# Latent heads inside a decoder trunk: the value slice moves from ScalarE to VectorE, the squares are formed from the copy, and the copy gets a third buffer

## The chip, the cores and the metric

One core of a Trainium2 chip runs the whole program. A core has a matrix engine (TensorE, PE in the profile), a vector engine (VectorE, DVE), an activation engine (ScalarE, ACT) and a general one (GpSimd, POOL). Each works through its own list of instructions in order. They share an SBUF memory; matrix products land in PSUM, in banks of 128 partitions x 512 float32. DMA transfers are issued by SyncE (SP) and by ACT, each from its own queue, and run on 16 shared DMA engines. The metric is the device time of one execution in microseconds (us); lower is better.

## The reference

The reference is a trunk of four layers over 1024 tokens of width 1024 plus 16 meta tokens. The even layers hold two groups of eight attention heads side by side: latent heads, whose queries and keys come out of a low-rank compression, and forgetting heads. What the change touches is the head of the latent group, cut here:

```
q  = (rms_norm(c_q,  g_cq)  @ w_uq ).reshape(b, l, 8, 96)          # c_q  384 wide
kv = (rms_norm(c_kv, g_ckv) @ w_ukv).reshape(b, l, 8, 64 + 64)     # c_kv 256 wide
k_nope, v_mla = kv[..., :64], kv[..., 64:]
k  = concatenate([k_nope, broadcast(k_pe, 8 heads)], axis=-1)      # 96 wide
q  = rope_tail(rms_norm(q, g_q_mla), cos, sin)
k  = rope_tail(rms_norm(k, g_k_mla), cos, sin)
```

So for each token and head there is a product, a sum of squares over the head's columns, a scaling by its inverse root, and a rotation of the last 32 columns. The values are scaled by the latent norm alone. After the attention comes one output projection, then the MLP or convolution layers, which fill the rest of the time.

## The kernel before

The attention of the even layer runs head by head. `prep(h)` loads a head's operands: for a forgetting head `fox_prep` (L406) issues on SP a query tile, a key tile, two halves of a second key tile (all from `fop_d`, L410 to L413) and a row of decay terms copied to all partitions (from `frow_d`, L414), all into tiles named `op`. `softmax` (L451) lets PE write scores into a bank named `sc` (L72 is the helper that records every matmul), DVE take them out with the running minimum (L474), ACT form exponentials with their sum (L484), DVE the reciprocal of the sum (L485) and GpSimd the scaling (L486). `transposes` (L491) turns blocks of 128 x 128 on PE into bank `tr` (L505), which DVE (L509) or ACT (L511) copies out into `pt`; `values` (L515) multiplies by the values into bank `av`, and ACT copies that out and stores it in two DMAs (L527 to L532). There are three `sc` banks, three `tr` banks, one `av` bank and one bank named `pq`.

`latent_heads` (L569) is a generator. While the first seven forgetting heads are worked on (270 to 480 us), it is resumed between their pieces, at a rate set by a constant, so that its matmuls stand between theirs on PE. It goes twice over nine token tiles (eight of 128 tokens, one of 16): pass 0 makes the queries (3 blocks of the latent, 4 heads x 96 = 384 columns a group), pass 1 keys and values (2 blocks, 512 columns). For each token tile `turn` loads a piece of the latent on SP (L588, `cn`), transposes it on PE (L591) and splits it into a high part on ACT (L595, `cH`) and a remainder on DVE (L596, `cL`). Then come two groups per tile ("quads"). A group is 9 or 6 matmuls into the one `pq` bank, out of weights `mwH` and `mwL`. ACT then squares the bank into `mjk` (L619), copies it into `qk` (L620) and in pass 1 scales the value half into `vv` (L622); DVE sums the squares (L624). After both groups a short chain on DVE and ACT (L627 to L638; L630 and L631 on ACT) forms the inverse roots, GpSimd scales and rotates `qk` in place (L636 to L653), and ACT's DMA queue stores `qk` (L654) and `vv` (L641). The `qk` and `vv` tiles have two buffers: a tile can be written again when the store of two tiles back has landed.

The latent heads then load what was stored: `tokens` (L388 to L391) reads `qk_d` into tiles `tm` and `v_d` into `v` on SP. After them the output projection begins: `w_out` (L673) loads a block of weights (`woraw`), DVE casts it (L678, `woH`), and PE multiplies in `pq` banks.

The order on every engine is not the order of the code. A scheduler places all instructions by its own simulated timeline, so an edit in one generator moves instructions of other functions too. Each DMA is also given one of eight completion lanes in turn, over both queues, and waits until the lane's last transfer has landed; in the listings these are the waits named DMAHW.

Of the kernel before, what the change touches and what calls it, by code (L numbers as in the profile page):

```python
# [18 lines left out]
F32 = mybir.dt.float32  # L19
BF16 = mybir.dt.bfloat16  # L20
F32R = mybir.dt.float32r
AF = mybir.ActivationFunctionType
ALU = mybir.AluOpType
# [4 lines left out]
P = 128  # L28
# [38 lines left out]
def trunk(ctx: ExitStack, tc: tile.TileContext, a: dict, out: bass.AP):  # L67
    nc = tc.nc
    V, S, G, T = nc.vector, nc.scalar, nc.gpsimd, nc.tensor
# [39 lines left out]
    with ExitStack() as att:  # L109
# [5 lines left out]
        lat = ac.tile([P, 2, NTT], F32, name="lat")  # L115
# [23 lines left out]
        with ExitStack() as s1:  # L139
# [90 lines left out]
            def project(i, WH, WL, N):  # L230
                t0, m = TT[i]
                ps = bank("sc")[:m, :N]
                n = 0
                for k in range(KD):
                    for x, w in ((H, WH), (H, WL), (L, WH)):
                        mm(ps, x[k][:, t0:t0 + m], w[k], n == 0, n == 23)
                        n += 1
                return ps
# [11 lines left out]
            for i, (t0, m) in enumerate(TT):  # L250
                ps = part[i] if i < 7 else project(i, *W, 296)
# [28 lines left out]
            j = fp.tile([P, NTT, 32], F32, name="pesq", bufs=1)  # L280
# [11 lines left out]
            for i, (t0, m) in enumerate(TT):  # L292
                ps = project(i, *W, NQL)
# [13 lines left out]
            for i0, i1 in ((0, 4), (4, 8), (8, 9)):  # L307
                ps = bank("tr")
                n = 0
                for i in range(i0, i1):  # L310
                    m = TT[i][1]
# [31 lines left out]
            for w in range(2):  # L343
                W = weights(f"w_g{2 + w}", 512)
                for i, (t0, m) in enumerate(TT):
                    ps = project(i, *W, 512)
                    j = jk.tile([P, 512], F32, name="jk")[:m]
# [7 lines left out]
                    x = jk.tile([P, 512], F32, name="cr")[:m].rearrange("p (h d) -> p h d", d=64)  # L355
# [10 lines left out]
            for i, (t0, m) in enumerate(TT):  # L366
                ps = project(i, *W, 512)
                if late:
                    turn(*late.pop(0))
                x = jk.tile([P, 512], F32, name="cr")[:m]  # L370
# [198 lines left out]
        def latent_heads():  # L569
            with ExitStack() as st:  # L570
                mw = st.enter_context(tc.tile_pool(name="mw", bufs=2, reuse_waits="tile"))
                for which, (k0, K, d) in enumerate(((0, 3, 96), (3, 2, 64))):
# [27 lines left out]
                    for i, (t0, m) in enumerate(TT):  # L600
                        if i + 1 < NTT:
                            turn(i + 1)
                            yield
                        cH, cL = cs_[i]
                        qk = mw.tile([P, 8, 96], F32, name="qk")[:m]
                        ss = small.tile([P, 8], F32, name="mss")[:m]
                        if which:
                            vv = mw.tile([P, 512], F32, name="vv")[:m]
                        for quad in range(2):
                            ps = bank("pq")[:m, :n4]  # L610
                            n = 0
                            for k in range(K):
                                for x, w in ((cH, WH), (cH, WL), (cL, WH)):
                                    mm(ps, x[:, k], w[:, k, quad * n4:quad * n4 + n4], n == 0, n == 3 * K - 1)
                                    n += 1
                            hs = slice(4 * quad, 4 * quad + 4)
                            x = ps[:, :4 * d].rearrange("p (h d) -> p h d", d=d)
                            j = mw.tile([P, NQL], F32, name="mjk")[:m, :4 * d].rearrange("p (h d) -> p h d", d=d)
                            S.activation(out=j, in_=x, func=AF.Square)  # L619
                            S.copy(out=qk[:, hs, :d], in_=x)  # L620
                            if which:
                                S.activation(out=vv[:, 256 * quad:256 * quad + 256], in_=ps[:, 256:512], func=AF.Copy,  # L622
                                             scale=lat[:m, 1, i:i + 1])
                            V.tensor_reduce(out=ss[:, hs], in_=j, axis=AX.X, op=ALU.add)  # L624
                            yield

                        V.tensor_scalar(out=ss, in0=ss, scalar1=lat2[:m, which, i:i + 1], scalar2=spe[:m, which, i:i + 1],  # L627
                                        op0=ALU.mult, op1=ALU.add)
                        y, t, rr = [small.tile([P, 8], F32, name="m" + n)[:m] for n in "ytr"]
                        S.activation(out=y, in_=ss, func=AF.Ln)  # L630
                        S.activation(out=y, in_=y, func=AF.Exp, scale=-0.5)  # L631
                        V.tensor_tensor(out=t, in0=y, in1=y, op=ALU.mult)
                        V.tensor_tensor(out=t, in0=t, in1=ss, op=ALU.mult)
                        V.tensor_scalar(out=t, in0=t, scalar1=-0.5, scalar2=1.5, op0=ALU.mult, op1=ALU.add)
                        V.scalar_tensor_tensor(out=rr, in0=y, scalar=lat[:m, which, i:i + 1], in1=t, op0=ALU.mult, op1=ALU.mult)
                        G.tensor_tensor(out=qk[:, :, :d], in0=qk[:, :, :d], in1=rr.unsqueeze(2).broadcast_to([m, 8, d]), op=ALU.mult)  # L636
                        if which:
                            V.tensor_tensor(out=rr, in0=y, in1=t, op=ALU.mult)  # L638
                            G.tensor_tensor(out=qk[:, :, 64:96], in0=kpe[:m, i, :].unsqueeze(1).broadcast_to([m, 8, 32]),
                                            in1=rr.unsqueeze(2).broadcast_to([m, 8, 32]), op=ALU.mult)  # L640
                            nc.scalar.dma_start(out=v_d[1].rearrange("r p i d -> p r i d")[:m, :, i],  # L641
                                                in_=vv.rearrange("p (r d) -> p r d", d=P))
                        else:
                            x1, x2 = qk[:, :, 64:80], qk[:, :, 80:96]
                            tb = [tab[0][:m, i, n, :].unsqueeze(1).broadcast_to([m, 8, 16]) for n in range(4)]
                            t1 = mw.tile([P, 8, 16], F32, name="t1")[:m]
                            t2 = mw.tile([P, 8, 16], F32, name="t2")[:m]
                            G.tensor_tensor(out=t1, in0=x2, in1=tb[2], op=ALU.mult)
                            G.tensor_tensor(out=t2, in0=x1, in1=tb[3], op=ALU.mult)
                            G.tensor_tensor(out=x1, in0=x1, in1=tb[0], op=ALU.mult)  # L650
                            G.tensor_tensor(out=x2, in0=x2, in1=tb[1], op=ALU.mult)
                            G.tensor_tensor(out=x1, in0=x1, in1=t1, op=ALU.subtract)
                            G.tensor_tensor(out=x2, in0=x2, in1=t2, op=ALU.add)  # L653
                        nc.scalar.dma_start(out=qk_d[which].rearrange("h p i d -> p h i d")[:m, :, i], in_=qk)  # L654
                        yield
# [96 lines left out]
        for m in PAIRS[:4]:  # L752
            x = op_.tile([P, 342], F32, name="hf", bufs=6)
            nc.scalar.dma_start(out=x, in_=h_d[m][:, 0:342])
            first[m] = x
        for n, m in enumerate(first):
            w = w_out(m, 0)
            ps = bank(("sc", "pq", "sc", "sc")[n])[:, :342]
# [28 lines left out]
    def bank_(w):  # L787
        return mp.tile([P, 512], F32, name="mp")[:, :w]
# [194 lines left out]
    for m in PAIRS:  # L983
        w = w_out(m, 0)
        for c0, c1 in ALL[m in first:]:
            ps = bank_(342)
# [232 lines left out]
```

## Time and profile before

| | |
|---|---|
| median of 3 runs | 2543.8 us (2543.32 to 2549.25) |
| the profiled execution | 2543.92 us, span 2542.2 us |
| mean granted TensorE clock | 0.982 |
| PE busy | 2428.5 us, 96% of the span |
| DVE, ACT, POOL busy | 1571.7, 807.8, 920.0 us |
| the latent stage, 270 to 480 us | PE busy 190.1 of 210, DVE 146.3, ACT 122.5, POOL 97.6 |

A row of the timeline gives the start, the duration, engine, line, operation, what is written and read, and in brackets the idle time of the engine just before and what ended it. "ACTq" and "SPq" rows are DMA issues on those queues. The duration of a matmul includes its latency, so matmuls that follow each other are read by the distance of their starts. A row of one line or tile gives the count and the least, median and greatest duration in nanoseconds. Rows of the DMA view give the number of transfers, the size of each and the time from issue to landing.

### The profile page before, as it was taken

How to read it: one execution, taken by the hardware profiler on the slowest of the kernel's cores; microseconds unless marked ns; L12 is line 12 of the kernel's file. 1: busy time of each engine (PE TensorE's matmuls, PEld its weight loads, DVE VectorE, ACT ScalarE, POOL GpSimd, SP SyncE). 2: the span in 40 equal slices, each digit the busy share in tenths (PEclk: the TensorE clock that was granted, in tenths of full speed). 3: DMA queues.
4: the chain of work that ended last, by engine and by line, in shares of the span. 5: the costliest groups of instructions: out<-in, count | busy, mean ns of one | idle time of the engine just before them, and what ended most of it. 6: DMA issues, size and time to landing. Idle time of an engine off the chain costs nothing.

```text
span 2542.2 us, 39452 instructions
## 1 busy us (share of the span) xinstructions
PE 2428.5 (96%) x15182; PEld 2162.6 (85%) x15182; DVE 1571.7 (62%) x3049; ACT 807.8 (32%) x1651; POOL 920.0 (36%) x694
## 2 busy tenths in 40 slices
PE   7999889999986999999999979999989999999999
PEld 7877676789886999999999969998868888888889
DVE  8573667665769666654544588778696556553432
ACT  3222456554635333320100252221353333210100
POOL 6353344532313333342423214445333334342420
PEclk9999999999998999999999989999999999999999
DMA  5234545444142333372312212225314334531311
GB/s 158 80 114 134 164 133 158 140 136 126 57 172 76 110 106 105 106 242 75 133 67 100 67 59 67 67 67 177 114 67 133 108 109 127 211 126 67 117 57 67
DMA packets 165645, 285.95 MB, mean 112 GB/s; under 512 B 35720, under 2 KB 104776, under 8 KB 165456
## 3 DMA queue, kind: packets, MB, share of 16 engines
q1 hardware_dynamic: 88608, 217.86, 26.8%
q10 hardware_dynamic: 76848, 65.56, 7.9%
q8 instruction: 120, 1.97, 0.3%
q14 instruction: 69, 0.57, 0.1%
HBM read 198.45 MB, written 84.91 MB: 111 GB/s over the span
## 4 chain that ended last, share of the span: by engine, by line
PE 79%; DVE 9%; DMA 6%; issue 4%; ACT 1%; POOL 1%; SPq 0%; ACTq 0%; DVEq 0%; POOLq 0%
PE mp L72 32%; PE mp L918 29%; PE sc L72 8%; PE pq L72 3%; PE av L72 3%; PE tr L505 3%; DVE lp L1143 1%; DMA qk_d<-qk 1%; DMA lp<-w_in_conv 1%; PE tr L439 1%; DMA lp<-w_up 1%; DVE hgL L178 1%; DVE pg L812 0%; DVE pg L809 0%; PE tr L333 0%
## 5 line engine op out<-in xcount | busy, mean ns | idle before, releaser
L918 PE MATMUL mp<-pg,lp 128*128 128x256 f32 (+2 forms) x5976 | 882.6, 310 | 39.9 <-ACT wk L941 10.7
L918 PEld LDWEIGHTS mp<-pg,lp 128*128 128x128 f32 x5976 | 818.1, 191 | 104.6 <-ACT wk L941 10.9
L72 PE MATMUL mp<-pg,lp 128*128 128x342 f32 (+2 forms) x4416 | 812.8, 346 | 0.7 <-DVE pg L1035 0.7
L72 PEld LDWEIGHTS mp<-pg,lp 128*128 128x128 f32 x4416 | 734.8, 189 | 77.8 <-DVE pg L1035 1.0
L910 POOL TENSOR_TENSOR lp<-lp 128x512 fp32r<-128x512 f32 x216 | 309.8, 1443 | 603.1 <-ACT lp L909 602.2
L1057 DVE TENSOR_TENSOR pg<-pg,mp 128x342 f32<-128x342 f32 (+2 forms) x368 | 206.8, 570 | 366.4 <-PE mp L72 366.2
L1046 POOL TENSOR_TENSOR lp<-lp 128x1024 fp32r<-128x1024 f32 x72 | 185.1, 2571 | 444.9 <-PE mp L72 382.4
L909 ACT CAST lp<-lp 128x512 fp32r<-128x512 f32 x303 | 179.3, 617 | 412.9 <-DVE lp L895 262.2
L1034 ACT CAST pg<-pg 128x1024 fp32r<-128x1024 f32 (+1 forms) x72 | 75.8, 1053 | 531.9 <-DMA pg<-hid 488.9
L486 POOL TENSOR_SCALAR Sb<-Sb,ls 128x144 f32<-128x144 f32 (+7 forms) x128 | 97.3, 765 | 194.2 <-DVE ls L485 118.1
L895 DVE TENSOR_TENSOR lp<-lp 128x512 f32<-128x512 f32 x86 | 72.4, 846 | 124.1 <-DMA lp<-w_up 84.3
L72 PE MATMUL sc<-op 128*128 128x264 f32 (+11 forms) x600 | 141.2, 349 | 6.4 <-DMA op<-fop_d 5.1
L72 PE MATMUL sc<-wH,hgH 128*128 128x512 f32 (+5 forms) x328 | 122.0, 378 | 8.9 <-DVE wH L150 7.6
L1095 ACT ACTIVATE wk<-wk 128x258 f32<-128x258 f32 (+1 forms) x192 | 92.3, 488 | 116.0 <-DVE wk L1093 106.5
L72 PE MATMUL sc<-wH,hgL 128*128 128x512 f32 (+5 forms) x328 | 122.4, 377 | 6.0 <-DVE hgL L178 6.0
L72 PE MATMUL sc<-wL,hgH 128*128 128x512 f32 (+5 forms) x328 | 121.4, 374 | 0.0
L505 PE MATMUL tr<-ident,Sb 128*128 128x128 f32 x704 | 117.7, 283 | 2.2 <-ACT pt L511 0.7
L1045 DVE CAST lp<-lp 128x1024 fp32r<-128x1024 f32 x72 | 97.0, 1347 | 33.9 <-DMA lp<-w_down 30.5
L1035 POOL TENSOR_TENSOR pg<-pg 128x1024 fp32r<-128x1024 f32 (+1 forms) x36 | 94.1, 2616 | 38.8 <-ACT pg L1034 38.7
L72 PEld LDWEIGHTS sc<-op 96*128 96x128 f32 (+1 forms) x600 | 94.2, 193 | 13.7 <-issue 6.8
L910 DVE TENSOR_TENSOR lp<-lp 128x512 fp32r<-128x512 f32 x87 | 82.4, 948 | 33.8 <-ACT lp L909 31.7
L505 PEld LDWEIGHTS tr<-ident,Sb 128*128 128x128 f32 x704 | 84.6, 144 | 15.3 <-issue 3.6
(287 smaller groups left out, 3004.8 us busy)
## 6 DMA issues: line engine op xcount, KB each, us to landing
lp<-w_down SPq DMA_DIRECT2D x64, 512.0 KB, 4.5
lp<-w_up SPq DMA_DIRECT2D x62, 512.0 KB, 4.8
pg<-hid SPq DMA_DIRECT2D x40, 512.0 KB, 5.0
pg<-hid SPq DMA_DIRECT2D x32, 514.0 KB, 5.1
hid<-wk ACTq DMA_DIRECT2D x64, 256.0 KB, 2.6
res<-pg SPq DMA_DIRECT2D x24, 514.0 KB, 3.5
pg<-res SPq DMA_DIRECT2D x24, 514.0 KB, 7.0
lp<-w_in_conv SPq DMA_DIRECT2D x24, 512.0 KB, 4.5
```

The source lines that it names most:

```text
L72: T.matmul(ps, lhsT=l, rhs=r, start=first, stop=last)
L486: G.tensor_scalar(out=sb[:, :nk], in0=sb[:, :nk], scalar1=ls, scalar2=1.0, op0=ALU.mult, op1=ALU.mult)
L505: T.transpose(ps[:, P * (b - b0):P * (b - b0) + P], sb[:, P * b:P * b + P], ident)
L909: S.copy(out=w[:, :512], in_=src)
L910: (V if i in (3, 7) else G).tensor_tensor(out=w[:, 512:], in0=src, in1=f(w)[:, :512], op=ALU.subtract)
L918: T.matmul(ps, lhsT=wt.W[i][:, y, k], rhs=o.N[k][i][:, x, c0:c1], start=start and k == 0 and n == 0, stop=k == 3 and n == 2, skip_group_ch ...
L1034: S.copy(out=h, in_=q)
L1035: (V if m % 2 else G).tensor_tensor(out=l, in0=q, in1=f(h), op=ALU.subtract)
L1045: V.tensor_copy(out=h, in_=q)
L1046: G.tensor_tensor(out=l, in0=q, in1=f(h), op=ALU.subtract)
L1057: V.tensor_tensor(out=hT[m][:, c0:c1], in0=hT[m][:, c0:c1], in1=ps, op=ALU.add)
L1095: S.activation(out=q, in_=q, func=AF.Square)
```

## The change

In `latent_heads` three things are edited. The `qk` tile gets three buffers. In pass 1 the value half of the bank is scaled by DVE (`tensor_scalar`), ahead of the copy, where ACT did it as the last of three. And the squares are formed by ACT from the `qk` tile in SBUF behind the copy, where they were formed from the bank ahead of it.

```
-                        qk = mw.tile([P, 8, 96], F32, name="qk")[:m]
+                        qk = mw.tile([P, 8, 96], F32, name="qk", bufs=3)[:m]
...
                             j = mw.tile([P, NQL], F32, name="mjk")[:m, :4 * d].rearrange("p (h d) -> p h d", d=d)
-                            S.activation(out=j, in_=x, func=AF.Square)
+                            if which:
+                                V.tensor_scalar(out=vv[:, 256 * quad:256 * quad + 256], in0=ps[:, 256:512],
+                                                scalar1=lat[:m, 1, i:i + 1], scalar2=None, op0=ALU.mult)
                             S.copy(out=qk[:, hs, :d], in_=x)
-                            if which:
-                                S.activation(out=vv[:, 256 * quad:256 * quad + 256], in_=ps[:, 256:512], func=AF.Copy,
-                                             scale=lat[:m, 1, i:i + 1])
+                            S.activation(out=j, in_=qk[:, hs, :d], func=AF.Square)
                             V.tensor_reduce(out=ss[:, hs], in_=j, axis=AX.X, op=ALU.add)
```

In the new kernel the value scaling is L620, the copy L622 and the square L623. The scheduler's order moves from about 290 us on to the end of the attention. Three places follow.

On ACT, around the store of the second query tile and the first copy into the fourth. A row shows the line, the operation, what is written and read, the size, and what it waits for. Before:

```order
L654 DMA qk_d0_98<-qk_2865 128x8x96 [waits DMAHW6_49,Pool_49]
L511 COPY pt_3131<-tr_3224 128x128 [waits PE_49]
L619 ACTIVATE mjk_3215<-pq_3205 128x384 [waits PE_49]
L511 COPY pt_3129<-tr_3263 128x2x128 [waits PE_49]
L630 ACTIVATE my_3137<-mss_3032 128x8 [waits DVE_49]
L484 ACTIVATE Sb3_2571,ls_3320<-Sb3_2571,nm_3318 128x1040 [waits DVE_49]
L484 ACTIVATE Sb4_2572,ls_3358<-Sb4_2572,nm_3356 128x144 [waits DVE_49]
L631 ACTIVATE my_3137<-my_3137 128x8 [waits Activation_49]
L484 ACTIVATE Sb5_2573,ls_3422<-Sb5_2573,nm_3420 128x272 [waits DVE_49]
L620 COPY qk_3203<-pq_3205 128x384 [waits DMAHW6_49]
```

After:

```order
L654 DMA qk_d0_98<-qk_2710 128x8x96 [waits DMAHW1_49,Pool_49]
L484 ACTIVATE Sb1_2569,ls_3199<-Sb1_2569,nm_3197 128x784 [waits DVE_49]
L527 COPY mixo_3094<-av_3074 128x256 [waits PE_49]
L622 COPY qk_3031<-pq_3098 128x384 [waits PE_49]
L530 DMA mix_d4_92<-mixo_3094 64x2x128 [waits DMAHW2_49,Activation_49]
L532 DMA mix_d4_92<-mixo_3094 64x256 [waits DMAHW4_49]
L623 ACTIVATE mjk_3108<-qk_3031 128x384 [waits Activation_49]
L595 CAST cH_3178<-tr_3174 128x384 [waits PE_49]
L654 DMA qk_d0_98<-qk_2865 128x8x96 [waits DMAHW5_49,Pool_49]
L484 ACTIVATE Sb2_2570,ls_3254<-Sb2_2570,nm_3252 128x912 [waits DVE_49]
L622 COPY qk_3203<-pq_3205 128x384 [waits DMAHW1_49,PE_49]
```

Before, the copy into the tile `qk_3203` waits for the store of `qk_2865`, nine rows ahead (lane 6); now it waits for that of `qk_2710`, ten rows ahead (lane 1). The tile `qk_2710` is the first, `qk_2865` the second, `qk_3203` the fourth.

On SP, the loads of one forgetting head (`op_4229` to `op_4232`) and what stands around them; `tm0` tiles are loads of the stored latent queries. Before:

```order
L410 DMA op_4229<-fop_d0_96 128x1040 [waits DMAHW2_49,PE_49]
L411 DMA op_4230<-fop_d1_97 128x1040 [waits DMAHW3_49,PE_49]
L412 DMA op_4231<-fop_d1_97 64x1040 [waits DMAHW4_49]
L413 DMA op_4231<-fop_d1_97 64x1040 [waits DMAHW5_49]
L414 DMA op_4232<-frow_d_86 128x1040 [waits DMAHW7_49,DVE_49]
L588 DMA cn_4348<-c_d_87 128x256 [waits DMAHW0_49,PE_49]
L588 DMA cn_4468<-c_d_87 128x256 [waits DMAHW6_49,DMAHW1_49,PE_49]
L588 DMA cn_4633<-c_d_87 128x256 [waits DMAHW5_49,DMAHW0_49,PE_49]
L390 DMA tm0_5489<-qk_d0_98 128x768 [waits DMAHW6_49,DMAHW4_49]
L390 DMA tm0_5786<-qk_d0_98 128x768 [waits DMAHW7_49]
```

After:

```order
L410 DMA op_4229<-fop_d0_96 128x1040 [waits DMAHW4_49,PE_49]
L411 DMA op_4230<-fop_d1_97 128x1040 [waits DMAHW6_49,DMAHW5_49,PE_49]
L412 DMA op_4231<-fop_d1_97 64x1040 [waits DMAHW6_49]
L413 DMA op_4231<-fop_d1_97 64x1040 [waits DMAHW7_49]
L390 DMA tm0_5489<-qk_d0_98 128x768 [waits DMAHW3_49,DMAHW0_49]
L390 DMA tm0_5786<-qk_d0_98 128x768 [waits DMAHW1_49]
L588 DMA cn_4348<-c_d_87 128x256 [waits DMAHW2_49,PE_49]
L588 DMA cn_4468<-c_d_87 128x256 [waits DMAHW4_49,PE_49]
L414 DMA op_4232<-frow_d_86 128x1040 [waits DMAHW6_49,DVE_49]
```

The two loads of latent queries, which wait for the stores of the seventh and eighth query tile, moved ahead of the head's row load, and so did two `cn` loads. The row load now waits on lane 6, which the load of the first half of `op_4231` holds.

On DVE, at the first weight cast of the output projection. Before:

```order
L474 ISA Sb0_2568,mx_5831<-sc_5832,zmask_460 128x400 [waits PE_49]
L474 ISA mx_5831 128x1
L678 CAST woH_6143<-woraw_6141 128x512 [waits DMAHW4_49,DMAHW2_49,DMAHW5_49,DMAHW1_49,DMAHW0_49]
L485 RECIPROCAL ls_5769<-ls_5769 128x1 [waits Activation_49]
L443 SCALAR_TENSOR_TENSOR op_5638<-tr_5718,gmla_444,op_5637 96x16 [waits Activation_49]
L509 COPY pt_5745<-tr_5773 128x3x128 [waits PE_49]
L485 RECIPROCAL ls_5798<-ls_5798 128x1 [waits Activation_49]
L474 ISA Sb1_2569,mx_5887<-sc_5888,zmask_460 128x264 [waits Pool_49]
```

After:

```order
L509 COPY pt_5745<-tr_5773 128x3x128
L509 COPY pt_5745<-tr_5802 128x3x128 [waits PE_49]
L474 ISA Sb2_2570,mx_5920<-sc_5921,zmask_460 128x328 [waits Pool_49]
L474 ISA mx_5920 128x1
L485 RECIPROCAL ls_5837<-ls_5837 128x1 [waits Activation_49]
L474 ISA Sb2_2570,mx_5920<-sc_5926,zmask_460,mx_5920 128x328 [waits DVE_49,PE_49]
L474 ISA mx_5920 128x1
L485 RECIPROCAL ls_5898<-ls_5898 128x1 [waits Activation_49]
L678 CAST woH_6143<-woraw_6141 128x512 [waits DMAHW6_49]
```

The cast of `woH_6143` now stands behind the evictions of two more pairs of score tiles, the reciprocals `ls_5769`, `ls_5798`, `ls_5837` and `ls_5898` and the copies into `pt_5745`, all of which followed it before.

## The prediction

> **What bounds the kernel now.** I read the busy shares first, then the chain of waits, then stretches of time.
>
> ```profile
> PE 2428.5 (96%) x15182; PEld 2162.6 (85%) x15182; DVE 1571.7 (62%) x3049; ACT 807.8 (32%) x1651; POOL 920.0 (36%) x694
> PE 79%; DVE 9%; DMA 6%; issue 4%; ACT 1%; POOL 1%; SPq 0%; ACTq 0%; DVEq 0%; POOLq 0%
> ```
>
> TensorE (PE) works 96% of the span, and 79% of the chain is its own work. The change touches only the latent heads, which run as filler inside the forgetting heads from 270 to 480 us. By stretch (columns: start and end, length, busy time of PE, its weight loads, DVE, ACT, POOL, then granted clock, DMA share, GB/s):
>
> ```profile
> 270.00:480.00 210.00, 190.12 (x1349) 147.65 (x1349) 146.26 (x557) 122.53 (x346) 97.60 (x140) 0.97 0.52 148
> 320.00:340.00 20.00, 20.00 (x132) 17.21 (x132) 12.55 (x46) 9.76 (x27) 6.99 (x11) 0.86 0.18 49
> 340.00:360.00 20.00, 17.01 (x124) 14.42 (x123) 12.88 (x57) 11.89 (x34) 8.91 (x14) 1.00 0.68 180
> 480.00:500.00 20.00, 16.24 (x105) 14.17 (x104) 11.70 (x45) 10.72 (x26) 11.26 (x10) 0.83 0.77 239
> ```
>
> PE stands for 19.9 us of the 210, so an edit here can bring no more than that and some clock. The largest standstill is the one below (PE rows; the bracket is the idle time before, and its releaser):
>
> ```profile
> 313.98 0.88 PE L505 MATMUL tr<-ident,Sb 128*128 128x128 f32 x6
> 319.66 0.69 PE L72 MATMUL pq<-mwH,cH 128*128 128x384 f32 x1 [4.80 <-ACT qk L620]
> 320.14 0.53 PE L72 MATMUL pq<-mwL,cH 128*128 128x384 f32 x1
> 322.38 0.53 PE L72 MATMUL pq<-mwH,cL 128*128 128x384 f32 x1
> ...
> 325.96 0.34 PE L72 MATMUL pq<-mwL,cH 128*128 128x384 f32 x1
> 326.14 0.35 PE L72 MATMUL pq<-mwH,cL 128*128 128x384 f32 x1
> ```
>
> PE ends at 314.86 and waits 4.80 us for the copy that frees the only "pq" bank. Behind it matmuls come 0.32 us apart (seven steps in 2.24), 6 us later 0.18: the clock has dropped, and the stretch's 0.86 says that 0.14 x 20 = 2.8 us of clock went. The nine matmuls of the group alone lose 9 x 0.14 = 1.3. I count 2.4. The copy is late for a store:
>
> ```profile
> 308.12 0.40 ACTq L654 DMA_DIRECT2D qk_d<-qk  x1
> 319.12 0.48 ACT L620 COPY qk<-pq 128x384 f32<-128x384 f32 x1 [5.34 <-DMA qk_d<-qk]
> ```
> ```profile
> 308.18 0.32 SPq L410 DMA_DIRECT2D op<-fop_d  x1
> ```
> ```profile
> qk_d<-qk ACTq DMA_DIRECT2D x1, 384.0 KB, 11.0
> DMA to landing us min/median/max: 2.9/3.1/11.0
> ```
>
> The store of an earlier qk tile left 0.06 us before the next head's five loads, shared the DMA engines with them and took 11.0 us in place of 3.1. With two buffers the copy into that tile waits for it.
>
> **The change, part by part.**
>
> *Engines.* Per group the rows are (median ns in the middle; the last is a DVE copy out of PSUM of the size that the value slice has):
>
> ```profile
> L619 ACT ACTIVATE mjk<-pq x36: 358/430/498, 282.5 to 472.4; 128x384 f32<-128x384 f32 x16, 128x256 f32<-128x256 f32 x16, 16x384 f32<-16x384 f32 x2, 16x256 f32<-16x256 f32 x2
> L620 ACT COPY qk<-pq x36: 344/422/488, 282.9 to 472.7; 128x384 f32<-128x384 f32 x16, 128x256 f32<-128x256 f32 x16, 16x384 f32<-16x384 f32 x2, 16x256 f32<-16x256 f32 x2
> L622 ACT ACTIVATE vv<-pq,lat x18: 461/490/504, 394.3 to 472.9; 128x256 f32<-128x256 f32 x16, 16x256 f32<-16x256 f32 x2
> ```
> ```profile
> L509 DVE COPY pt<-tr 128x256 f32<-128x256 f32 x8 | 3.3, 417 | 1.1 <-PE tr L505 1.0
> ```
>
> ACT loses 18 x 0.49 = 8.8 us, DVE gains 18 x 0.42 = 7.5: 154 of 210, its idle time covers it. The trace has no square out of SBUF; I take 0.43 as before (bounds: 0.37 and 0.49). It now follows the copy that it reads, and such a pair on ACT can leave a hole:
>
> ```profile
> 340.57 0.21 ACT L631 ACTIVATE my<-my 128x8 f32<-128x8 f32 x1 [0.46 <-ACT my L630]
> 403.51 0.16 DVE L485 RECIPROCAL ls<-ls 128x1 f32<-128x1 f32 x1 [3.05 <-ACT Sb L484]
> ```
>
> 36 holes of 0.46 would be 16.6 us, beside 87 in which ACT stands: off PE's path. The bank is held for 0.42 in place of 0.43 + 0.42 in the query pass, and for 0.42 + 0.42 in place of 1.34 in the key pass, where the copy carries a wait for DVE: the two engines read one after the other. So the engines earn nothing by themselves, 0 us. But DVE's value step now stands behind whatever DVE waits for (the second row: 3.05 us for an exponential), and ACT's copy, the squares and exponentials behind it, and PE's next group stand behind that. I add 1.0 us for new waits; bounds 0 and two of 2.1, 4.2.
>
> *Place A, 314.86.* In the new order the copy behind which PE waited is preceded by the store of two tiles back, which left ACT ten rows earlier and was issued well before the loads. The 4.80 and the 2.4 go. Late next are the loads of the next head:
>
> ```profile
> 341.85 0.32 SPq L410 DMA_DIRECT2D op<-fop_d  x1
> ```
> ```profile
> 347.28 0.49 PE L505 MATMUL tr<-ident,Sb 128*128 128x128 f32 x3
> 350.70 0.72 PE L72 MATMUL sc<-op 128*128 128x256 f32 x3 [2.94 <-DMA op<-fop_d]
> ```
>
> There the first score comes 350.70 - 341.85 = 8.85 us after the first load, behind 5.91 us of other work. At A PE has 314.86 - 308.18 = 6.68 of work since the loads, and the waiting group adds 9 x 0.18 = 1.6: 8.3, by the rows of the new order about 0.6 less. A wait of 8.85 - 7.7 = 1.2 appears. **A = -4.80 - 2.4 + 1.2 = -6.0**; ends -7.2 (no wait) and -4.3 (2.94).
>
> *Place B, 350.70.* The new order has one more group of nine ahead of this score: 2.94 falls by 1.6. **B = -1.6**; ends 0 and -2.9.
>
> *Place C, the head loaded at 368.79.*
>
> ```profile
> 368.79 0.32 SPq L410 DMA_DIRECT2D op<-fop_d  x1
> 370.98 0.37 SPq L414 DMA_DIRECT2D op<-frow_d  x1
> 394.05 1.56 SPq L390 DMA_DIRECT2D tm<-qk_d  x2
> ```
> ```profile
> 375.50 0.71 PE L72 MATMUL sc<-op 128*128 128x256 f32 x3 [0.37 <-DMA op<-fop_d]
> 377.71 0.36 PE L72 MATMUL sc<-op 128*128 128x256 f32 x1 [1.12 <-DMA op<-fop_d]
> ```
> ```profile
> 381.07 0.16 DVE L420 TENSOR_TENSOR bias<-op,zmask 16x16 f32<-16x16 f32 x1
> ```
> ```profile
> op<-fop_d SPq DMA_DIRECT2D x2, 260.0 KB, 9.0
> op<-frow_d SPq DMA_DIRECT2D x1, 520.0 KB, 9.7
> ```
>
> Here the score loses a group ahead of it: +1.6. And on SP the two tm loads, now issued at 394.05 when the last full query store has landed, stand ahead of this head's row load (L414), with two cn loads between, and the row load also waits for a K load that lands about 9 us after its issue. The tm loads add 0.8 MB to 2.1 MB that take 9.7 us: 2.7 if all of it delays the K loads; I take half, 1.4. **C = +3.0**; ends 0 and +4.3 with a cold clock of 2.4 on top. The row load would leave at about 378 and land at 382 to 384, and L420, which reads it, stood at 381.07 and comes some 20 DVE rows later now: nearly covered.
>
> *Place D.* The tm loads leave this place:
>
> ```profile
> 404.54 0.50 PE L72 MATMUL pq<-mwH,cH 128*128 128x512 f32 x1 [2.11 <-ACT vv L622]
> ```
>
> ACT's copy of vv was the releaser, and is gone, but DVE takes its part. **D = -1.0**; ends -2.1 and +2.1. Two heads on, one group fewer ahead of the score, with no wait before: **+0.5**; ends 0 and 1.6.
>
> *Place E, the start of the output projection.*
>
> ```profile
> 489.18 0.08 DVE L474 DVE_READ_ACCUMULATOR2_ANT mx<- 128x1 f32 x1
> 492.74 0.43 DVE L678 CAST woH<-woraw 128x512 fp32r<-128x512 f32 x1 [3.48 <-DMA hf<-xT]
> ```
> ```profile
> 493.31 0.63 PE L72 MATMUL pq<-mixH,woH 128*128 128x342 f32 x1 [3.17 <-DVE ls L485]
> ```
>
> DVE stands at the first weight cast, and the reciprocals behind it hold up PE; 0.17 x 20 = 3.4 us of clock go with it. In the new order four score evictions, four reciprocals and two transposed blocks more come ahead of that cast. If the load keeps its time the hole closes; if it moves too, nothing changes. Of 3.17 + 2.9 I take half: **E = -3.0**; ends 0 and -6.1.
>
> *The sum:* -6.0 - 1.6 + 3.0 - 1.0 + 0.5 - 3.0 + 1.0 = **-7.1 us**. The profiled execution took 2543.92 us (span 2542.2 and 1.7 around it), 0.1 over the median of 2543.8; so 2536.8.
>
> On the clock, standstills of 3.17 and 4.80 us were followed by a slow stretch and the one of 2.94 was not (0.86 and 0.83 against 1.00). The Trainium skill, "TensorE: Matmul & The Clock Gate", Part 1, says that the clock halves after an idle window of about 3.4 us that runs freely; the trace agrees roughly, and by that rule a wait of 2.9 at A or C could chill or not by chance, 2.4 us either way.
>
> The Trainium skill, "PSUM — Partial Sum Buffer", section "PSUM bank collisions raise a hardware error", says that two engines may not touch one bank and quadrant at once, and that a dependency is put between them, for two readers too. By it the bank is never read by both at the same time and nothing is earned from overlap; the copy's wait for DVE agrees, and the sum holds nothing for it.
>
> **The rivals.**
>
> *R1, the load wait takes the place whole.* A costs 2.94 anew and E and D keep their holes: -4.3 - 1.6 + 3.0 + 0.5 + 1.0 = -1.4, 2542.5. For it: 350.70 is just such a wait. Against: A has 2 us more work than B had.
>
> *R2, both chilled holes close and C is covered.* -7.2 - 2.9 - 6.1 + 1.6 + 1.0 = -13.6, some 2530. For it: only these two holes chill the clock. Against: the weight loads at E may move as well.
>
> *R3, SP's order at C (slower).* If the query store lands late, the tm loads hold SP, and cn and row loads behind them; DVE stands at L420 in its order, evictions and transposes stop, PE stops. For each us that the row load leaves after 380, PE loses about one, with 2.4 of clock from 3.2 on. Left at 390, between 378 and the 394.05 of the tm loads: 10 + 2.4 in place of the 3.0, so -7.1 + 9.4 = +2.3, 2546; left at 394 and with the cn loads late, +6 to +10, 2552. Against: ACT's row for that store now stands ahead of an exponential that ran at 367.
>
> *R4, the value step.* Three waits of 3.2 with 2.4 of clock each through DVE's order: -7.1 + 16.8 = +9.7, 2553.5. It decides from the second on. For it: the 3.05 at 403.51. Against: one in the trace.
>
> **The numbers.** A run of this kernel tells 0.3%, 7.6 us, from no change. Forecast (-3.5 to -10.5) 0.42, of it 0.18 beyond 7.6; R1 0.15; R2 0.24; R3 0.12, half of it slower by over 0.3%; R4 0.07. Faster 0.18 + 0.24 = 0.42; slower 0.06 + 0.07 = 0.13, less 0.01 for R4's mild form: 0.12; the same 0.46. The range 2530 to 2548 holds the forecast, R1, most of R2 and half of R3; the likeliest alone spans 2533.5 to 2540.5.
>
> **What would show it.** A: no PE wait over 3 us between 305 and 325, the granted clock near 1.00 there, a wait for op of 0.5 to 3 us in its place. B: under 2 us. C: a wait for op of 2 to 5 us, the tm loads some 20 us earlier; DVE idle at L420 over 3 us would show R3. E: DVE's idle time ahead of L678 under 2 us and a clock over 0.95 from 480 to 500. Key pass: copies that wait for DVE; PE gaps over 3 us released by them would be R4. The prediction falls if PE's idle time from 270 to 500 doesn't shrink by 3 us or more, or if the gain comes from ACT's or DVE's busy time.

## The result and the profile after

The changed kernel took 2532.8 us in the median of five runs (2529.2 to 2535.5), beside 2549.3 us for the kernel before on the same chip (2543.3 to 2551.7): a ratio of 0.9944, 95% interval 0.9932 to 0.9957. That is 14 us, twice the 7.1 forecast and past the 0.3%. A second series, told below as e5, gave 0.9941 (0.9929 to 0.9953). The profiled execution took 2535.49 us with a span of 2533.8; it is the longest of its five, while the profile of before was near the short end of its runs. The two profiles are 8.4 us apart, and the rows below explain no more than that by themselves.

The first rows of the page, and the stretches that the prediction showed, of the kernel after:

```profile
PE 2426.6 (96%) x15182; PEld 2161.0 (85%) x15182; DVE 1580.0 (62%) x3067; ACT 804.7 (32%) x1633; POOL 918.7 (36%) x694
```
```profile
270.00:480.00 210.00, 194.79 (x1432) 153.81 (x1432) 159.05 (x613) 125.74 (x345) 98.97 (x146) 0.99 0.55 155
320.00:340.00 20.00, 19.11 (x137) 15.49 (x136) 14.71 (x56) 10.69 (x31) 13.48 (x25) 1.00 0.36 95
340.00:360.00 20.00, 18.88 (x142) 15.95 (x142) 15.21 (x60) 13.46 (x38) 12.08 (x21) 1.00 0.72 196
480.00:500.00 20.00, 18.54 (x128) 13.83 (x128) 13.84 (x39) 12.94 (x26) 15.12 (x11) 0.99 0.72 232
```

In the latent stage PE stands for 15.2 us instead of 19.9 and works through 1432 matmuls instead of 1349. The two stretches with a clock of 0.86 and 0.83 now have 1.00 and 0.99. More work falls into the same 210 us, so ACT shows 125.7 us there against 122.5; over the stretch of equal work below it is busy 3.5 us less, and DVE 6.0 more.

The larger PE waits after, by place (timeline rows of PE):

```profile
275.75 1.54 PE L591 MATMUL tr<-ident,cn 128*128 128x128 f32 x6 [3.39 <-DMA cn<-c_d]
...
320.87 0.65 PE L72 MATMUL sc<-op 128*128 128x256 f32 x3
...
350.26 0.75 PE L72 MATMUL sc<-op 128*128 128x256 f32 x3 [0.30 <-DMA op<-fop_d]
352.48 0.36 PE L72 MATMUL sc<-op 128*128 128x256 f32 x1 [0.81 <-DMA op<-fop_d]
...
374.63 0.72 PE L72 MATMUL sc<-op 128*128 128x256 f32 x3 [0.62 <-DMA op<-fop_d]
377.19 0.36 PE L72 MATMUL sc<-op 128*128 128x256 f32 x1 [0.21 <-DMA op<-fop_d]
...
400.93 0.72 PE L72 MATMUL sc<-op 128*128 128x256 f32 x3 [0.53 <-DMA op<-fop_d]
403.19 0.59 PE L72 MATMUL sc<-op 128*128 128x256 f32 x3 [0.83 <-DMA op<-fop_d]
...
476.86 0.22 PE L439 MATMUL tr<-ident,tm 16*96 16x16 f32 x1 [1.60 <-DMA tm<-qk_d]
...
485.74 0.42 PE L72 MATMUL pq<-mixH,woH 128*128 128x342 f32 x1 [0.39 <-DVE woH L678]
```

The stall of 4.80 is gone, and the first score of the next head (320.87) follows without a wait. No gap of the stage after 276 reaches 2 us.

To compare whole kernels, take the stretch from the first exponential of the forgetting heads to the first matmul of the MLP. Every kernel here does the same 3483 to 3485 matmuls in it. Columns as before (start and end, length, PE busy and so on, clock third from the end); before, and then after:

```profile
265.20:782.40 517.20, 478.84 (x3483) 400.42 (x3483) 351.58 (x1140) 277.13 (x693) 196.32 (x245) 0.97 0.46 136
```
```profile
266.70:772.90 506.20, 474.57 (x3483) 397.13 (x3482) 357.54 (x1158) 273.58 (x675) 193.33 (x245) 0.98 0.47 139
```

The stretch is 11.0 us shorter: 6.7 less of PE standing (38.4 to 31.6) and 4.3 less of PE busy with the same work. The clock record has four stretches of 3.41 us at half speed fewer (six and two, from 270 to 530 us), which would be up to 6.8 us. The stretch begins 1.5 us later, and what follows it takes 1760.9 instead of 1759.8, which leaves 8.4.

### The profile page after: what moved, and what is told of

Its sections match the earlier page's. It is cut to its first block, busy times and chain, and to the rows that moved or that the text cites. A ratio compares the mean times of both kernels' runs of the same rounds, so it can differ in the third digit from the quotient of the medians.

```text
span 2533.8 us, 39431 instructions
## 1 busy us (share of the span) xinstructions
PE 2426.6 (96%) x15182; PEld 2161.0 (85%) x15182; DVE 1580.0 (62%) x3067; ACT 804.7 (32%) x1633; POOL 918.7 (36%) x694
## 4 chain that ended last, share of the span: by engine, by line
PE 65%; DVE 8%; DMA 4%; issue 2%; ACT 1%; POOL 0%; ACTq 0%; SPq 0%; DVEq 0%; POOLq 0%
PE mp L72 32%; PE mp L918 26%; PE sc L72 2%; PE pq L72 2%; PE av L72 2%; PE tr L505 1%; DVE lp L1143 1%; DMA lp<-w_up 1%; DMA lp<-w_in_conv 1%; DVE pg L812 1%; DMA mixr<-mix_d 1%; DVE lp L895 1%; DVE lp L903 1%; PE tr L439 1%; DVE pg L809 1%
## 5 line engine op out<-in xcount | busy, mean ns | idle before, releaser
L918 PE MATMUL mp<-pg,lp 128*128 128x256 f32 (+2 forms) x5976 | 883.8, 310 | 35.8 <-ACT wk L941 10.7
L72 PE MATMUL sc<-wH,hgH 128*128 128x512 f32 (+5 forms) x328 | 122.5, 380 | 8.8 <-DVE wH L150 7.6
L910 DVE TENSOR_TENSOR lp<-lp 128x512 fp32r<-128x512 f32 x87 | 80.7, 928 | 32.7 <-ACT lp L909 30.4
```

Of the source, the lines that this page charges most:

```text
L72: T.matmul(ps, lhsT=l, rhs=r, start=first, stop=last)
L910: (V if i in (3, 7) else G).tensor_tensor(out=w[:, 512:], in0=src, in1=f(w)[:, :512], op=ALU.subtract)
L918: T.matmul(ps, lhsT=wt.W[i][:, y, k], rhs=o.N[k][i][:, x, c0:c1], start=start and k == 0 and n == 0, stop=k == 3 and n == 2, skip_group_ch ...
```

## The experiments

Six kernels make the eight combinations of the three edits complete. The others move the weight cast, add a fourth buffer, or change the pace of the filler. Each was timed against the kernel before on the same chip, five rounds each. The median of before was 2543.95 beside e1 to e4, 2545.44 beside e5 to e8, 2546.84 beside e9 to e12. "Idle" and "busy" are PE's in the stretch above, in one profiled execution; that one is not always typical (e8's took 2541.86 us where the median is 2550.45, e11's 2536.74 against 2543.41, e7's 2564.08 against 2559.76), so the ratios are what to compare, and idle and busy time only roughly. "last cn" is the last transpose of the latent filler, in us after that stretch's start.

| run | buffers | squares from copy | values on DVE | ratio (95%) | idle, busy | last cn |
|---|---|---|---|---|---|---|
| before | 2 | no | no | 1 | 38.4, 478.8 | 187.3 |
| e1 | 3 | no | no | 0.9973 (0.9959 to 0.9987) | 31.5, 476.7 | 178.9 |
| e7 | 2 | yes | no | 1.0049 (1.0036 to 1.0063) | 44.8, 490.3 | 197.5 |
| e8 | 2 | no | yes | 1.0018 (1.0008 to 1.0028) | 35.1, 478.3 | 183.0 |
| e2 | 2 | yes | yes | 1.0042 (1.0030 to 1.0054) | 39.8, 483.5 | 186.7 |
| e4 | 3 | yes | no | 0.9948 (0.9936 to 0.9960) | 31.6, 470.9 | 175.1 |
| e6 | 3 | no | yes | 0.9966 (0.9954 to 0.9979) | 33.4, 471.3 | 175.4 |
| e5, the change | 3 | yes | yes | 0.9941 (0.9929 to 0.9953) | 31.9, 472.0 | 173.3 |
| e9 | 4 | yes | yes | 0.9950 (0.9936 to 0.9964) | 30.7, 474.3 | 174.5 |
| e3, cast on ACT | 2 | no | no | 0.9997 (0.9985 to 1.0008) | 34.7, 473.4 | 181.1 |
| e10, pace 1.6 | 2 | no | no | 1.0053 (1.0039 to 1.0067) | 41.5, 488.6 | 170.7 |
| e11, pace 1.6 | 3 | yes | yes | 0.9986 (0.9976 to 0.9995) | 32.7, 477.3 | 154.8 |
| e12, pace 1.15 | 3 | yes | yes | 0.9974 (0.9956 to 0.9993) | 39.0, 474.4 | 179.1 |

**e1: the third buffer alone.**

```
-                        qk = mw.tile([P, 8, 96], F32, name="qk")[:m]
+                        qk = mw.tile([P, 8, 96], F32, name="qk", bufs=3)[:m]
```

> Third buffer for qk alone; value scaling and squares stay as before. Two-holes theory (the gain is the stall of 4.80 us at 314.86 with its slow clock, 7.2 us, and, apart from it, the hole at the first weight cast, 3.17 with its slow clock, 6.1 us): the copy waits for the store of two tiles back, so the first hole goes and the load wait at 350.70 shrinks (-1.5 to -3); the cast stands as early on DVE as before, so the second hole stays or shrinks little. -7 to -10 us, no PE gap over 3 us between 305 and 325, a gap of 2 to 4 us ahead of the first output product. Bank-earlier theory (the gain comes from the bank being freed sooner by the copy): within 2 us of before. Drawn-anew theory (the parts do not add, the scheduler's order decides): anything between -14 and +5, with holes at new places.

The median was 2537.2 against 2543.95, -6.8 us, but the runs spread from 2527.6 to 2542.9. The first hole goes:

```profile
ACT qk L620 <- DMA qk_d<-qk: 3.2, 1, 3.2
```
```profile
322.14 0.45 PE L72 MATMUL pq<-mwH,cH 128*128 128x384 f32 x1 [0.74 <-ACT qk L620]
...
374.49 0.72 PE L72 MATMUL sc<-op 128*128 128x256 f32 x3 [3.24 <-DMA op<-fop_d]
...
481.62 0.40 PE L72 MATMUL pq<-mixH,woH 128*128 128x342 f32 x1 [0.95 <-DVE ls L485]
```

One copy still waits 3.2 us for a store, where five waited 8.2 us before; of it 0.74 reaches PE. The hole at the first output product is 0.95 here although the weight cast stands as early on DVE as before. That part of the two-holes theory, that the cast's place in the line keeps the hole open, did not hold. The bank-earlier theory had the buffer alone within 2 us of before, and the interval (-3.6 to -10.4 us) excludes that.

**e2: values and squares moved, two buffers.** Against the changed kernel:

```
-                        qk = mw.tile([P, 8, 96], F32, name="qk", bufs=3)[:m]
+                        qk = mw.tile([P, 8, 96], F32, name="qk")[:m]
```

> Value scaling on DVE and squares from the copy, but two buffers. Two-holes theory: the copy still waits for the store of the tile just before, so the stall at 314.86 stays, 3 to 5 us with its slow clock; the cast stands late on DVE as in the change, so the second hole goes: -5 to -7 us. Bank-earlier theory: -10 to -14 us, the whole gain. Drawn-anew theory: neither, holes at new places.

It was 10.7 us slower by the ratio, against both numbers that were put down; only the third theory, that the parts don't add, allows it. The stall at 314.86 is not there either, so the scheduler's new order removed it without the buffer: the store of the second tile left 1.7 us ahead of the next head's loads and took 3.3 us. Other waits came:

```profile
398.09 0.72 PE L72 MATMUL sc<-op 128*128 128x256 f32 x3 [3.56 <-DMA op<-fop_d]
...
434.49 0.72 PE L72 MATMUL sc<-op 128*128 128x256 f32 x3 [2.41 <-DMA op<-fop_d]
...
488.91 1.06 PE L439 MATMUL tr<-ident,tm 128*96 128x128 f32 x4 [3.53 <-DMA tm<-qk_d]
```

The last is a wait for the load of stored latent keys: the filler ends 8 to 13 us later than with three buffers and the latent heads find its output not yet there. A late filler is not enough to explain it, since before ends as late (187.3) and has no such wait.

**e3: the weight cast on ACT, latent heads as before.**

```
-            V.tensor_copy(out=h, in_=raw)
+            S.copy(out=h, in_=raw)
```

> The latent heads as before; only the cast of the output weights' high part is done by ACT in place of DVE. The order up to 485 us stays nearly as before. Two-holes theory: the stall at 314.86 stays (4 to 5 us), the hole at 490 on DVE and PE goes if DVE's place in line was its cause: -4 to -7 us; if the weight load itself is late, ACT stands in place of DVE and its exponentials and copies hold up PE: -1 to +3 us. Bank-earlier theory: within 2 us.

No difference: 0.9997, medians 2543.35 and 2543.95, runs from 2537 to 2552. In its profile the long wait at the first output product is not there, and in its place PE waits at other points of the output projection:

```profile
318.09 0.45 PE L72 MATMUL pq<-mwH,cH 128*128 128x384 f32 x1 [3.41 <-ACT qk L620]
...
489.67 0.77 PE L505 MATMUL tr<-ident,Sb 128*128 128x128 f32 x5 [1.53 <-ACT pt L511]
...
510.10 0.43 PE L72 MATMUL pq<-mixH,woH 128*128 128x342 f32 x1 [1.24 <-ACT mixH L668]
```

So closing that hole by itself was not shown to be worth anything; ACT's waits took its place in part, and the run cannot tell how much.

**e4: third buffer and squares from the copy, values on ACT.**

```
+                        qk = mw.tile([P, 8, 96], F32, name="qk", bufs=3)[:m]
...
-                            S.activation(out=j, in_=x, func=AF.Square)
                             S.copy(out=qk[:, hs, :d], in_=x)
...
+                            S.activation(out=j, in_=qk[:, hs, :d], func=AF.Square)
```

> Third buffer and squares from the copy; the value scaling stays on ACT, between copy and square. Two-holes theory: the first hole goes, the cast stands early on DVE, so the second stays or shrinks: -7 to -10 us, within 2 us of the third buffer alone. Bank-earlier theory: -5 to -9 us more than the third buffer alone. Drawn-anew theory: no fixed relation to the third buffer alone, over 4 us apart with a hole that one has and the other has not.

It was 13.2 us faster (0.9948): 6.4 us of ratio more than the third buffer alone, and within the interval of the full change. That is the step that the bank-earlier theory had put down, but e1 and e2 had gone against that theory already; it is more than the two-holes theory allowed. It also fits the drawn-anew theory, as e1 has a wait of 3.24 us at 374.49 that e4 has not. Idle time is that of e1 (31.6 and 31.5); busy time is 5.8 us lower, of which one length at half clock fewer (two, not three) can be 1.7; the rest is not explained. No copy waits for a qk store in its profile.

**e5 to e8: the change again, and the remaining combinations.** e5 is the changed kernel. e7 is the kernel before with the first edit below, e8 with the second, e6 with the second and the third.

```
-                            S.activation(out=j, in_=x, func=AF.Square)
                             S.copy(out=qk[:, hs, :d], in_=x)
...
+                            S.activation(out=j, in_=qk[:, hs, :d], func=AF.Square)
```
```
+                            if which:
+                                V.tensor_scalar(out=vv[:, 256 * quad:256 * quad + 256], in0=ps[:, 256:512],
+                                                scalar1=lat[:m, 1, i:i + 1], scalar2=None, op0=ALU.mult)
                             S.activation(out=j, in_=x, func=AF.Square)
                             S.copy(out=qk[:, hs, :d], in_=x)
-                            if which:
-                                S.activation(out=vv[:, 256 * quad:256 * quad + 256], in_=ps[:, 256:512], func=AF.Copy,
-                                             scale=lat[:m, 1, i:i + 1])
```
```
+                        qk = mw.tile([P, 8, 96], F32, name="qk", bufs=3)[:m]
```

> The changed kernel again, beside the single edits on one chip. All theories: -10 to -15 us.

> Third buffer and value scaling on DVE; squares still from the bank, ahead of the copy. Third-buffer theory (the store's wait leaves the copy, the latent pass runs ahead of the heads, and no PE wait for loads or stores grows past the 3.4 us that chill the clock): -7 to -14 us, the span from the first exponential of the forgetting heads to the start of the MLP 502 to 510 us against 517, the last latent transpose by 446 us. Squares theory (third buffer with squares from the copy brought 13, third buffer alone 7: the squares are worth 6): -5 to -8, less than the change by 5. Drawn-anew theory: anything from -14 to 0.

> Squares from the copy alone, two buffers, value scaling on ACT. Third-buffer theory: 0 to +8 us as with squares and value scaling together (+10), since the copy waits for the store before it; the last latent transpose near 453 us, a PE wait over 3 us for a load or a store. Squares theory: -5 to -7. Drawn-anew theory: -8 to +10.

> Value scaling on DVE alone, two buffers, squares from the bank. The order up to 370 us is that of before, so the stall at 314.86 stays (3 to 5 us) in every theory. Third-buffer theory: -4 to +5 us. Squares theory: +3 to +5, the value scaling being the loss in squares and value scaling together (+10). Drawn-anew theory: -8 to +10.

e5 repeated the gain, -15 us by the ratio. e6 gave -8.7 (-5.3 to -11.7 by the interval), which fits both the squares theory (-5 to -8) and the third-buffer theory's range. e7, the squares alone, was 12.5 us slower by the ratio, which the squares theory excludes and which is more than the +8 that the third-buffer theory allowed. e8 was 4.6 us slower, inside what both theories gave it. Its stall is where it was:

```profile
318.68 0.69 PE L72 MATMUL pq<-mwH,cH 128*128 128x384 f32 x1 [4.69 <-ACT qk L623]
...
479.28 0.98 PE L439 MATMUL tr<-ident,tm 128*96 128x128 f32 x4 [3.30 <-DMA tm<-qk_d]
```

and e7 shows what the squares do without the buffer:

```profile
401.73 1.22 PE L72 MATMUL sc<-op 128*128 128x256 f32 x3 [3.45 <-DMA op<-fop_d]
...
498.28 1.06 PE L439 MATMUL tr<-ident,tm 128*96 128x128 f32 x4 [5.59 <-DMA tm<-qk_d]
```
```profile
265.40:800.50 535.10, 490.31 (x3483) 407.92 (x3483) 355.75 (x1140) 281.22 (x693) 193.43 (x245) 0.95 0.45 132
```

The same matmuls are busy 11.5 us longer than before, at a clock of 0.95, and PE stands 6.4 us longer, in an execution 4.3 us above the median.

The eight combinations together: the mean ratio of the four kernels with three buffers is 0.9957 (with 0.9943 for the change), of the four with two 1.0027. The buffer is worth 0.70%, 18 us, on the mean, but it depends on the others: 0.27% alone, 0.52% with the values on DVE, 1.01% with the squares from the copy, 0.99% with both. Squares from the copy bring -0.24% (6 us) with three buffers and cost +0.37% (9 us) with two. The values on DVE give -0.06% with three and +0.06% with two. They bring nothing in any pair that is clear of the intervals; alone (e8) they cost 0.18%, with an interval just above 1.

**e9 to e12: is it the store's wait or the filler's head start?**

```
e9   qk = mw.tile(..., bufs=4)      in the changed kernel
e10  LR = 1.6  (was 1.3)            in the kernel before
e11  LR = 1.6                       in the changed kernel
e12  LR = 1.15                      in the changed kernel
```

> The change with four buffers for qk in place of three; the order of instructions on PE and ACT is that of the change around the first copies, the copy there waits for no store at all. Store-wait theory (the gain is that the copy no longer waits for the store just before it, three buffers being enough): within 2 us of the change, -12 to -16 us. If waits for stores are still left with three: 2 to 5 us better than the change.

> The kernel before, with the pace of the latent filler raised from 1.3 to 1.6 steps, two buffers, nothing else. Run-ahead theory (what counts is that the latent pass ends early, so that the loads of what it stored are not waited for): -5 to -10 us. Store-wait theory: the pass meets the same two buffers with less time between tiles, so copies wait for stores at more places: 0 to +10 us, PE gaps ended by the copy or by loads of 2 to 5 us.

> The change with the pace raised from 1.3 to 1.6. Run-ahead theory: 2 to 5 us better than the change. Store-wait theory: no relation to the pace as long as no wait over 3.4 us appears: -8 to -16 us against before.

> The change with the pace lowered from 1.3 to 1.15, so that the latent pass ends later, three buffers. Run-ahead theory: most of the gain is lost, -4 to +3 us against before, with a PE wait of 3 us or more for the load of stored latent keys. Store-wait theory: -8 to -14 us, that wait being under 3 us.

A fourth buffer adds nothing (0.9950 beside 0.9941 and 0.9944), as the store-wait theory said: with three, no copy waited for a qk store in the profile of the change.

e10 is the clearest case against the head start alone. The filler ends 17 us earlier than before and no load of stored keys is waited for; the kernel is 13.5 us slower by the ratio, with the rows below and one of 2.73 left at the first output product:

```profile
347.92 1.22 PE L72 MATMUL sc<-op 128*128 128x256 f32 x3 [3.77 <-DMA op<-fop_d]
380.56 1.12 PE L72 MATMUL sc<-op 128*128 128x256 f32 x3 [2.78 <-DMA op<-fop_d]
...
526.14 0.42 PE L72 MATMUL pq<-mixH,woH 128*128 128x342 f32 x1 [2.87 <-ACT mixH L668]
```

But its copies wait for stores for 3.1 us in all, less than the 8.2 before, so the store's wait does not explain it either; the waits are for loads. e11 lost most of the gain at the faster pace (0.9986, -3.6 us), where the head-start theory said it would grow and the store-wait theory that it would stay. e12, slowed, kept 6.6 us, between what the two theories said, and has the long wait that the head-start theory named:

```profile
472.85 1.09 PE L439 MATMUL tr<-ident,tm 128*96 128x128 f32 x4 [6.35 <-DMA tm<-qk_d]
```

So neither theory covers all runs. What holds: with three buffers at the old pace no copy holds up PE by more than 1.6 us, and every kernel with two buffers has, after 290 us, a PE wait of 3.4 us or more for a copy or a load; of the five with three or four buffers at that pace one has a wait over 3 us there (e1, 3.24). At which loads the others wait differs with the scheduler's order. Why that order turns out worse with two buffers stays open.

## Why the prediction was right, and where it was off

The direction and the range held: 2532.8 lies in 2530 to 2548. The likeliest case said -7.1; what came is nearest the rival R2, to which I gave 0.24. Some of that is luck. The kernel before took 2549.3 us beside it, not the 2543.8 from which I counted; 0.9944 of 2543.8 would be 2529.6, just below the range. And I had given "the same" 0.46 and "faster" 0.42. The sign that would have made the prediction fall did not come: PE's idle time from 270 to 500 us went from 23.6 to 16.7 us. By the steps, with the rows of the two profiles:

*Place A, said -6.0, was -7.2.* The 4.80 and the clock went, but by more than the buffer. In the kernel after, the store of the second tile, the first copy into the fourth, and the next head's first load:

```profile
310.92 0.38 ACTq L654 DMA_DIRECT2D qk_d<-qk  x1
...
313.16 0.46 ACT L622 COPY qk<-pq 128x384 f32<-128x384 f32 x1
```
```profile
313.47 0.32 SPq L410 DMA_DIRECT2D op<-fop_d  x1
```

The store now left 2.55 us ahead of the loads and not 0.06, and took 4.3 us and not 11.0. It landed 2.1 us after the copy began, so in this order a copy with two buffers would have stood some 2.1 us (an estimate from these rows) in place of 5.34. The prediction did not see that the store itself would be quicker. The other runs agree: where the loads left within 0.3 us behind this store (before, e1, e3, e6, e8) it took 9.8 to 12.8 us; where they left 1.7 to 2.6 us behind it (e2, e4, e5, e7, the change) 3.0 to 4.8. The second group is the kernels with the squares from the copy, so that edit, too, removes the stall. Another store was slow:

```profile
DMA to landing us min/median/max: 2.7/3.0/9.4
```

The 9.4 is that of the sixth tile, issued at 345.84, and nobody waits for it. The new wait of 1.2 that I put in its place did not come, since the head's loads were quicker than at the place from which I took 8.85 us: the first load left at 313.47 and the score began at 320.87, 7.4 us later. That the third buffer takes away this stall where the store is slow is shown by e1 (the store took 12.4 us, 0.74 of the stall left), beside before and e8, where it stays without the buffer.

*Place B, said -1.6, was -1.8:* 2.94 became 0.30 + 0.81.

*Place C, said +3.0, was -0.7.* This is the step that failed. The order was read rightly:

```profile
368.57 0.32 SPq L410 DMA_DIRECT2D op<-fop_d  x1
...
370.62 1.09 SPq L390 DMA_DIRECT2D tm<-qk_d  x2
372.44 0.86 SPq L588 DMA_DIRECT2D cn<-c_d  x2
375.88 0.32 SPq L414 DMA_DIRECT2D op<-frow_d  x1
```
```profile
382.56 0.17 DVE L420 TENSOR_TENSOR bias<-op,zmask 16x16 f32<-16x16 f32 x1 [0.99 <-DMA op<-frow_d]
```

The tm loads left 23 us earlier, and the row load 5 us later than before and 2 us earlier than I put it; DVE stood 0.99 us for it, as good as covered. But neither the group that left the place nor the shared loads cost anything: the score began 6.06 us after the first load, sooner than the 6.71 of before, though 0.8 MB more was on the way. I had charged the added bytes at the mean rate of the loads; the loads that the score waits for were issued ahead of the tm loads, which may be why, but that was not tested.

*Place D, said -1.0, was -1.5:* 2.11 + 0.71 became 0.53 + 0.83. Two heads on, said +0.5, was +0.6 (0.20 and 0.38, where before had no wait).

*Place E, said -3.0, was about -5.6* in the two profiles (3.17 to 0.39, and nearly all of the clock). The mechanism that I gave, more work on DVE ahead of the cast, is seen in the row below, where DVE stands 1.22 instead of 3.48. It is not what decides: e1 closed the hole with the cast in its old place, and e3 closed it without gaining. I count the size as seen in one pair of profiles and the cause as open. (E's sum took 2.9 us of clock where the line before it works out 3.4.)

```profile
485.25 0.43 DVE L678 CAST woH<-woraw 128x512 fp32r<-128x512 f32 x1 [1.22 <-DMA woraw<-w_out_attn]
```

*New waits, said +1.0:* the 1.60 at 476.86 for stored keys, 1.0 more at the first latent transpose (3.39 against 2.35), and 1.2 at the loads of the head that begins near 293 (0.48 and 0.70): about +3.8. The sum of these is -7.2 - 1.8 - 0.7 - 1.5 + 0.6 - 5.6 + 3.8 = -12.4, beside the -11.0 measured over the stretch. Two lengths at half clock are not in it and cancel: the one at 281 us is gone, one at 477 came.

*The engines, said 0:* there was no gain, in e6 against e1 or in e8 against before. e8 was 0.18% slower, with an interval that lies just above 1 (1.0008 to 1.0028). The rows for the new operations (squares, then values):

```profile
L623 ACT ACTIVATE mjk<-qk x36: 399/474/536, 284.9 to 462.3; 128x384 f32<-128x384 f32 x16, 128x256 f32<-128x256 f32 x16, 16x384 f32<-16x384 f32 x2, 16x256 f32<-16x256 f32 x2
L620 DVE TENSOR_SCALAR vv<-pq,lat x18: 462/475/486, 376.9 to 460.2; 128x256 f32<-128x256 f32 x16, 16x256 f32<-16x256 f32 x2
```

A square out of SBUF takes 0.47, against 0.43 out of the bank, inside my bounds; the value step on DVE 0.48, where I had 0.42 from a plain copy. ACT stood 2.0 us in all ahead of the squares, four times, not 16.6. Copies waited for the value step four times, 2.6 us in all, and of that PE saw little (0.5 us behind copies): R4 did not come. R3 did not come either. The two engines read the bank one after the other: in all 18 groups the copy began 33 ns or more behind the end of the value step.

What the prediction missed is the interaction. It costed the parts as independent, with 0 for the squares; alone they cost 12.5 us, and with the buffer they bring 6. Why they bring 6 is not shown. It also looked for the gain in idle time and at two holes; in fact 4.3 of the 11.0 is busy time, and what e4 has over e1 in the profiles is busy time alone (5.8). R2's reason, that only two holes chill the clock, was not right either: before has lengths at half clock at 274 and 281 us as well.

## What to carry to other kernels

A tile that is stored to memory and then written again waits for the slowest store, not for the median one (3.1 and 11.0 us here): a buffer more is cheap, and it has to be priced by the longest landing in the trace and by what was issued just behind that store; here moving the store 2 us away from the loads took the stall away as well. Under a scheduler that places everything, an edit must be tried together with the resource that it needs: the same squares were +9 us with two buffers and -6 with three. And of two profiles of kernels that do the same matmuls, compare idle and busy time of PE over one stretch with fixed ends; the single gaps move about, and here they did not add up to the result by themselves.

## What the runs showed of the hardware

The granted clock of PE is recorded in stretches of 3.41 us and small multiples of it, at 0.5 of full speed. From 270 to 530 us there are six such lengths in the profile of before, two in that of the change, eleven in e7. In each profile they begin on one raster of 3.41 us (before: 274.4, 281.2, 318.7 and 492.8 us, that is 2, 13 and 64 lengths after the first). Which wait is followed by one does not go by its length alone: 2.35 us (before, at 273), 1.84 us (e4, at 477) and 1.60 us (after, at 477) were, 2.94 (before, at 351) was not. How the wait falls on the raster explains it: of the 2.35 us, 2.21 stood in one length; the 2.94 was split, and the two lengths had 1.70 and 1.29 us of standing. In the fourteen profiles, from 270 to 530 us, a length in which PE stood 1.74 us or more was always followed by one at half clock. With 1.60 to 1.73 us it went either way, and below that half clock came only straight behind another such length, but for one case (e7, at 442, with 1.12). It agrees with a window that runs freely, as the Trainium skill, "TensorE: Matmul & The Clock Gate", Part 1, has it, but the 3.4 us that it names is the length of the window and not the wait that is needed: about half of it was enough here. One length at half clock costs at most 1.7 us; the 2.4 that I used was for the two lengths behind the 4.80.

The median qk store of before landed after 3.1 us. Five copies waited for one, 8.2 us in all, and the stall came from the store that left 0.06 us ahead of five loads from another queue and took 11.0. The pairs of place A show how close is close: 0.3 us or less ahead of the loads cost some 7 to 10 us, 1.7 us or more at most 2. The store of 9.4 us in the change left 3.5 us behind such a first load (342.38 and 345.84), so leaving just behind the loads is slow too.
